# A hybrid S5 / convolution / mLSTM layer: first modulation weights loaded and multiplied ahead of the tokens' statistics, and the moves of the S5 inputs made steps of the S5 side job

## The chip, the core and the metric

The kernel runs on one core of one Trainium2 chip. The metric is the device time of a run in microseconds, and of several runs the median. A second measure is the span of one profiled execution, from its first to its last instruction.

Five engines work side by side, each through its own list of instructions in order: TensorE (PE in the rows, its weight loads PEld), VectorE (DVE), ScalarE (ACT), GpSimd (POOL) and SyncE (SP). SP and POOL only issue loads here, apart from a few clears. An instruction that waits holds up all that stands behind it on its engine.

## The reference, cut to what matters

One layer of a backbone with 256 latent tokens `x` and 256 context tokens `ctx`, each of 2048 features:

```
sh1, sc1, g1, sh2, sc2, g2 = split(silu(c) @ w_mod + b_mod, 6)      # for x with c, for ctx with c_ctx
hx = rmsnorm(x) * (1 + sc1) + sh1 ; hc the same of ctx              # statistics: mean of squares per token
zx = hx @ w_in + b_in ; zc = hc @ w_in + b_in                       # columns: S5, convolution, q, k, v, o, gates
mix = concat(s5_mixer(zc, zx), conv_module(zx), mlstm_mixer(zc, zx))
x = x + g1 * (mix @ w_out)
x = x + g2 * (swiglu(rmsnorm(x) * (1 + sc2) + sh2) @ w_ffn_out)
return rmsnorm(x)
```

The S5 mixer is a diagonal recurrence in two directions over 32 groups of 16 channels, first over the context, then over the tokens, with a GELU and a gated projection behind it. All inputs are float32.

## The kernel before

**Weights.** All weights of the matrix products are cut into tiles of 128 x 128 and stored in the order in which they are used, in chunks of eight tiles, 512 KB each. `raw_dma` (line 259) loads a chunk on SP into one of three `raw` buffers. `split` writes a high part `whi` (a cast by ScalarE, `acopy`, line 201) and the low rest `wlo` (a subtraction by VectorE, `tt`, line 168); there are three buffers of each. Every product is made of three matmuls (`mm3`): high with high, high with low, low with high. `nxt` hands out the tiles in order, fetches and splits ahead, and calls the planner. In the prediction, "`raw` 0" is the first chunk.

**The start.** SP loads the packed vectors (`pv`, `lam`), an identity (`cst`), the tokens `xr` (line 338) and the context `cr` (line 340) in four loads of 512 KB each, and then what the list `plan` says: the modulation weights of the first row tiles, `wm`, and the first weight chunks, by when they are needed. A row tile's modulation has four pieces of 512 KB. `wm_dma` (line 331) places piece number n in buffer n modulo 7: four buffers `wm` and three borrowed from tiles that are idle then (`wmu`, `wmt`, named for what lies there later). Pieces 0 to 6 are loaded by SP, later ones by POOL, and each of those has to wait until TensorE has multiplied the piece that lay in its buffer. `matvec_piece` multiplies a piece with the SiLU of the two condition vectors, `matvec_end` copies the sums out of PSUM (ScalarE), turns them with two transposes and adds them up into the shift and scale `as1` of one row tile (VectorE).

The statistics: ScalarE squares the tokens (two halves for each load), VectorE adds the two halves, TensorE adds over partitions by a matmul with ones into one bank (`stp`, tag `qk`), and `rsqrt` follows: a logarithm and an exponential on ScalarE and three VectorE operations (`stt`, line 179) that end in `rst`. `make_h` multiplies a row tile of tokens by `rst` and writes `hx` and `hc`, each as high and low part. Beside all this VectorE works through the S5 parameters (`wmt`, `LW`, `LC`, `s5c` in the rows), a side job of small operations.

**Phase 1** goes over the 16 row tiles. For each it multiplies the S5 columns and three tiles of the keys' columns for both streams, and in between makes the modulation and `h` of the next row tile. At its end ScalarE reads four PSUM banks out into `zT` (S5 inputs, features on partitions) and three into `kT` (keys).

**The S5 part.** `U` holds the S5 inputs in chunk layout. `s5_moves` fills it from `zT` by 16 copies of 32 partitions, eight on ScalarE and eight on VectorE (`vcopy`, line 183), written out at once before the S5 side job is added. `s5_job` prepares sixteen pairs of units (`prep`) and runs them (`main5`). `prep` transposes `Wb` (line 839) into a PSUM bank, copies it to `Wi`, then computes `M2` in another bank. `main5` multiplies `U` with `Wi`, scans on VectorE, and ends with matmuls of which the last reads `U` and `M2`. Behind the sixteenth pair come a GELU over `U`, sixteen ScalarE and sixteen VectorE copies into `gT` and a split into `gs`.

**What sets the order.** `Sched` writes TensorE's main work in order and slips steps of the side jobs in between: convolution, S5, attention, gates and the modulations that wait (`mod_job`; a few of these multiply on TensorE, `wm` with `cs`, and are turned at line 749). A side job is a generator, each `yield` ends a step, and `pump` starts steps by priority as long as the rough costs counted for VectorE and ScalarE are less than 3500 ns ahead of TensorE's. The framework then orders the instructions of each engine by its own estimate, except where the order is pinned, and puts in the waits. PSUM has three banks of tag `b`, which the convolution, the modulations, the S5 job and attention share.

Of the kernel before, what the change touches and what calls it, by code (L numbers as in the profile page):

```python
# [19 lines left out]
KT = 16  # L20
# [86 lines left out]
class Sched:  # L107
    """Emits the tensor engine's main work in order and slips steps of side jobs in between."""
# [42 lines left out]
def hybrid_layer_kernel(ctx: ExitStack, tc: tile.TileContext, xt, ctxt, wm1, wmr, wst, wg, bvrow, pvd, cstd, s5p, out):  # L151
# [155 lines left out]
    def rsqrt(o, ps, n, scale, eps, epsv):  # L307
        """o = 1/sqrt(ps*scale + eps), refined by one Newton step"""
# [25 lines left out]

    xr = pre.tile([128, KT, NT], F32, name="xr", tag="X")
# [7 lines left out]
    def load_gates():  # L343
# [5 lines left out]
    # the order of the loads that share the queue up to the end of phase 1: by when they are needed  # L349
    NP1 = (4 + KHEAD) * KT // CH  # L350
    plan = sorted([(8 * c / 7 - RAW_EARLY, 0, c) for c in range(NP1)] +
                  [(i // 4 - (MV_LEAD + 1) / 7 + (i % 4) * 0.01 if i >= 4 else -99, 1, i) for i in range(4 * KT)])
# [51 lines left out]

    lnexp()
    stp = bank("qk", 2)
# [11 lines left out]
    for q in range(4):  # L418
        matvec_piece(0, q)
        plan_pump()  # L420
    matvec_end(0)

# [18 lines left out]
    def s5_params():  # L441
# [43 lines left out]
        # half-angle sine and cosine  # L485
# [17 lines left out]
        # lambda_bar - 1 and its quotient by lambda  # L503
# [15 lines left out]
        # powers of lambda_bar  # L519
# [126 lines left out]
    def fourA(n, src, ps):  # L646
        """column tiles in turn, each over all rows: x tokens only"""
        for kt in range(KT):
            mm3(ps, nxt(), (src[:, kt, 0, :], src[:, kt, 1, :]), kt == 0, kt == KT - 1)
# [7 lines left out]
    def conv_job():  # L657
# [14 lines left out]
        def sum4(x):  # L672
            """sums over partitions and the four tiles, every partition the same"""
# [98 lines left out]
    U = pre.tile([128, 16, 128], F32, name="U", tag="U")  # L772
    def s5_moves():
        for s in range(4):
            for q in range(4):
                o = U[32 * s:32 * s + 32, q::4, :]
                i = zT[32 * q:32 * q + 32, :, s::4]
                if (s + q) % 2:
                    vcopy(o, i)
                else:  # L780
                    acopy(o, i)

    def s5_job():
# [111 lines left out]

        yield from prep(0)
        for p in range(16):
            a, b = main5(p), (prep(p + 1) if p < 15 else iter(()))
# [27 lines left out]
    s5_moves()  # L926
# [3 lines left out]
    # the convolution's columns  # L930
# [15 lines left out]
    def gates_job():  # L946
# [28 lines left out]
        # context columns: decay to the end of the context  # L975
# [204 lines left out]
    # last range, with the sums of squares for the second norm  # L1180
    A2 = sb.tile([128, 16], F32, name="A2")
    stt(A2, mods[:, 2, :], 1.0, pvc("n2g", 0, 16), OP.add, OP.mult)
    class SumSq:
        """sums of squares over features, every partition the same: four tiles at once while there is time"""
# [111 lines left out]
    for n in (1, 1, 2, 2, 2, 2, 2, 2, 2):  # L1296
# [3 lines left out]
        i += n  # L1300


# [1 line left out]
def pack(inp):  # L1304
    f = {k: np.asarray(v) for k, v in inp.items()}

# [103 lines left out]
```

## Time and profile before

| | |
|---|---|
| median of 3 runs | 1482.44 us (1481.68 to 1483.52) |
| span of the profiled execution | 1479.6 us (its own time beside the span is not listed) |
| TensorE busy | 1437.5 us, 97% |
| VectorE busy | 1005.1 us, 68% |
| ScalarE busy | 716.0 us, 48% |
| GpSimd busy | 107.2 us, 7% |
| chain that ended last | TensorE 89%, VectorE 5%, ScalarE 3%, DMA 1% |
| moved by the DMA engines | 315.56 MB, 213 GB/s on average |

TensorE is the engine that sets the time over nearly all of the span; its busy time is a sum over pipelined matmuls. In a timeline, a row is a group of like instructions that follow each other: where it starts, how long the group takes, engine, line, what is written and read, and how many. Brackets at the end give the engine's idle time ahead of the row and what ended it. A row of loads gives the time from issue to landing in its last column.

### The profile page before, as it was taken

How to read it: one execution, taken by the hardware profiler on the slowest of the kernel's cores; microseconds unless marked ns; L12 is line 12 of the kernel's file. 1: busy time of each engine (PE TensorE's matmuls, PEld its weight loads, DVE VectorE, ACT ScalarE, POOL GpSimd, SP SyncE). 2: the span in 40 equal slices, each digit the busy share in tenths (PEclk: the TensorE clock that was granted, in tenths of full speed). 3: DMA queues.
4: the chain of work that ended last, by engine and by line, in shares of the span. 5: the costliest groups of instructions: out<-in, count | busy, mean ns of one | idle time of the engine just before them, and what ended most of it. 6: DMA issues, size and time to landing. Idle time of an engine off the chain costs nothing.

```text
span 1479.6 us, 29243 instructions
## 1 busy us (share of the span) xinstructions
PE 1437.5 (97%) x11840; PEld 1351.2 (91%) x11840; DVE 1005.1 (68%) x1960; ACT 716.0 (48%) x1199; POOL 107.2 (7%) x207
## 2 busy tenths in 40 slices
PE   5999899999999999999899999999999999999996
PEld 3888788887888999999899999999999999999996
DVE  7555699988978887888776677455454554455554
ACT  4334776653565555645544444433444334443353
POOL 1221111110101110011000010000000000000000
PEclk9999999999999999999999999999999999999998
DMA  9997464442526666789477787555565555555553
GB/s 360 368 354 291 160 219 136 162 163 86 169 88 228 214 217 227 268 304 353 143 234 265 282 299 239 183 185 186 183 185 185 188 189 181 188 185 186 185 177 114
DMA packets 87943, 315.56 MB, mean 213 GB/s; under 512 B 10096, under 2 KB 10880, under 8 KB 87808
## 3 DMA queue, kind: packets, MB, share of 16 engines
q1 hardware_dynamic: 60912, 216.67, 44.1%
q0 software_dynamic: 26896, 97.02, 18.4%
q8 instruction: 93, 1.52, 0.4%
q14 instruction: 42, 0.34, 0.1%
HBM read 311.55 MB, written 2.10 MB: 212 GB/s over the span
## 4 chain that ended last, share of the span: by engine, by line
PE 89%; DVE 5%; ACT 3%; DMA 1%; issue 1%; SPq 0%; DVEq 0%; ACTq 0%
PE ps_m L208 70%; PE ps_b L208 13%; PE ps_qk L208 5%; DVE tmp L168 1%; DMA tmp<-in_wg_dram 1%; ACT tmp L195 0%; DMA raw<-in_wst_dram 0%; PE ps_b L839 0%; ACT whi L201 0%; ACT U L201 0%; DVE wlo L168 0%; DMA xr<-in_xt_dram 0%; ACT gT L201 0%; PE ps_b L749 0%; DVE tmp L191 0%
## 5 line engine op out<-in xcount | busy, mean ns | idle before, releaser
L168 DVE TENSOR_TENSOR wlo<-raw,whi 128x1024 fp32r<-128x1024 f32 x386 | 471.6, 1223 | 317.7 <-ACT whi L201 309.5
L201 ACT CAST whi<-raw 128x1024 fp32r<-128x1024 f32 x386 | 404.0, 1047 | 508.6 <-PE ps_m L208 373.8
L208 PE MATMUL ps_m<-h,whi 128*128 128x256 f32 x2624 | 470.4, 282 | 3.6 <-ACT h L195 3.6
L208 PEld LDWEIGHTS ps_m<-h,whi 128*128 128x128 f32 x2624 | 404.1, 189 | 4.0 <-ACT h L195 4.0
L208 PE MATMUL ps_m<-h,wlo 128*128 128x256 f32 x1312 | 370.0, 282 | 0.0
L208 PE MATMUL ps_m<-ffa,whi 128*128 128x256 f32 x1408 | 251.0, 281 | 0.0
L208 PEld LDWEIGHTS ps_m<-h,wlo 128*128 128x128 f32 x1312 | 247.8, 189 | 0.0
L208 PEld LDWEIGHTS ps_m<-ffa,whi 128*128 128x128 f32 x1408 | 215.7, 188 | 1.4 <-issue 1.2
L208 PE MATMUL ps_m<-ffa,wlo 128*128 128x256 f32 x704 | 197.2, 280 | 0.0
L208 PE MATMUL ps_m<-hx,whi 128*128 128x256 f32 x960 | 186.8, 290 | 5.5 <-ACT hx L195 3.6
L208 PEld LDWEIGHTS ps_m<-hx,whi 128*128 128x128 f32 x960 | 148.8, 190 | 24.8 <-issue 16.3
L179 DVE SCALAR_TENSOR_TENSOR macc<-wm,cs,macc 128x512 f32<-128x512 f32 x180 | 134.3, 746 | 6.6 <-ACT macc L195 5.1
L208 PE MATMUL ps_m<-hx,wlo 128*128 128x256 f32 x480 | 135.9, 284 | 0.0
L208 PEld LDWEIGHTS ps_m<-ffa,wlo 128*128 128x128 f32 x704 | 132.2, 188 | 0.0
L331 POOL DMA_DIRECT2D wm<-in_wmr_dram x128 | 67.5, 528 | 614.6 <-DVE macc L179 432.9
L208 PEld LDWEIGHTS ps_m<-hx,wlo 128*128 128x128 f32 x480 | 90.9, 190 | 0.2 <-DVE wlo L168 0.2
L179 DVE SCALAR_TENSOR_TENSOR xres<-ps_m,mods,xres 128x256 f32<-128x256 f32 x96 | 46.1, 481 | 35.0 <-PE ps_m L208 34.8
L179 DVE SCALAR_TENSOR_TENSOR XB<-XB,pv 128x256 f32<-128x256 f32 x120 | 53.7, 479 | 0.6
L208 PE MATMUL ps_m<-hc,whi 128*128 128x256 f32 x256 | 52.0, 284 | 0.0
L208 PE MATMUL ps_m<-mixm,whi 128*128 128x256 f32 x256 | 47.3, 286 | 0.0
L208 PE MATMUL ps_m<-whi,hx 128*128 128x512 f32 x128 | 46.5, 400 | 0.0
L201 ACT CAST ffa<-tmp 128x256 fp32r<-128x256 f32 x44 | 17.7, 405 | 49.6 <-DVE tmp L168 49.6
(267 smaller groups left out, 1997.3 us busy)
## 6 DMA issues: line engine op xcount, KB each, us to landing
raw<-in_wst_dram SPq DMA_DIRECT2D x386, 512.0 KB, 4.1
wm<-in_wmr_dram POOLq DMA_DIRECT2D x128, 512.0 KB, 5.2
wm<-in_wm_dram POOLq DMA_DIRECT2D x32, 512.0 KB, 7.2
wmu<-in_wm_dram POOLq DMA_DIRECT2D x16, 512.0 KB, 7.0
wmt<-in_wm_dram POOLq DMA_DIRECT2D x7, 512.0 KB, 6.4
wm<-in_wm_dram SPq DMA_DIRECT2D x5, 512.0 KB, 10.5
xr<-in_xt_dram SPq DMA_DIRECT2D x4, 512.0 KB, 6.6
cr<-in_ctxt_dram SPq DMA_DIRECT2D x4, 512.0 KB, 9.8
```

Of the source, the lines that this page charges most:

```text
L168: V.tensor_tensor(out=o, in0=a, in1=b, op=op)
L179: V.scalar_tensor_tensor(o, a, s, b, op0=op0, op1=op1)
L201: S.copy(o, a)
L208: i = P.matmul(o, lhsT=l, rhs=r, start=start, stop=stop, skip_group_check=sgc, **kw)
L331: i = (q or nc.gpsimd).dma_start(wm[key], src)
```

## The change

It has two parts. In the first, the loads of the four modulation pieces of row tile 0 are issued on SP ahead of the tokens, the planner's list starts with piece 4, and the multiplication of the four pieces and `matvec_end(0)` are written ahead of the statistics. The call of `plan_pump` behind each piece becomes one call behind all four. In the second, `s5_moves` becomes a generator `s5_move(q)` that makes four of the sixteen copies, with a `yield` behind each two and an extra 500 ns counted for each ScalarE copy; the S5 job runs `s5_move(0)` before the first preparation and `s5_move(1)` to `s5_move(3)` ahead of the first three pairs. The rest of the diff removes comments.

```diff
+    for q in range(4):
+        wm_dma((0, q), wm1[0, q], nc.sync)
     xr = pre.tile([128, KT, NT], F32, name="xr", tag="X")
     cr = sb.tile([128, KT, NT], F32, name="cr", tag="R1")
...
     plan = sorted([(8 * c / 7 - RAW_EARLY, 0, c) for c in range(NP1)] +
-                  [(i // 4 - (MV_LEAD + 1) / 7 + (i % 4) * 0.01 if i >= 4 else -99, 1, i) for i in range(4 * KT)])
+                  [(i // 4 - (MV_LEAD + 1) / 7 + (i % 4) * 0.01 if i >= 4 else -99, 1, i) for i in range(4, 4 * KT)])
...
+    for q in range(4):
+        matvec_piece(0, q)
     lnexp()
+    matvec_end(0)
+    plan_pump()
     stp = bank("qk", 2)
...
     rsqrt(rst, stp, 512, 1.0 / D, eps6, 1e-6)
-    for q in range(4):
-        matvec_piece(0, q)
-        plan_pump()
-    matvec_end(0)
-
...
-    def s5_moves():
+    def s5_move(q):
         for s in range(4):
-            for q in range(4):
-                o = U[32 * s:32 * s + 32, q::4, :]
-                i = zT[32 * q:32 * q + 32, :, s::4]
-                if (s + q) % 2:
-                    vcopy(o, i)
-                else:
-                    acopy(o, i)
+            o = U[32 * s:32 * s + 32, q::4, :]
+            i = zT[32 * q:32 * q + 32, :, s::4]
+            if (s + q) % 2:
+                vcopy(o, i)
+            else:
+                acopy(o, i)
+                sc.act += 500
+            if s % 2:
+                yield
...
+        yield from s5_move(0)
         yield from prep(0)
         for p in range(16):
+            if p < 3:
+                yield from s5_move(p + 1)
             a, b = main5(p), (prep(p + 1) if p < 15 else iter(()))
...
-    s5_moves()
     s5o = {}
     s5j = sc.add(s5_job(), P_S5)
```

The order of the built program moves in four places that matter here. The first is SP's queue at the start. Before, tokens and context stand ahead of the first modulation pieces:

```order
L231 DMA pv<-in_pvd_dram 128x377
L233 DMA lam<-in_pvd_dram 128x96
L235 DMA cst<-in_cstd_dram 128x128
L338 DMA xr<-in_xt_dram 128x1024 x4
L340 DMA cr<-in_ctxt_dram 128x1024 x4
L331 DMA wm<-in_wm_dram 128x1024 x4
L259 DMA raw<-in_wst_dram 128x1024
```

In the change:

```order
L231 DMA pv<-in_pvd_dram 128x377
L233 DMA lam<-in_pvd_dram 128x96
L235 DMA cst<-in_cstd_dram 128x128
L331 DMA wm<-in_wm_dram 128x1024 x4
L340 DMA xr<-in_xt_dram 128x1024 x4
L342 DMA cr<-in_ctxt_dram 128x1024 x4
L259 DMA raw<-in_wst_dram 128x1024
```

The four `wm` moved ahead of eight loads, which each come four places later; the first `raw` keeps its place.

The second is ScalarE behind the squares at the start, where the first activation of `ps_qk` is the logarithm of the statistics and the next the exponential. Before:

```order
L195 ACTIVATE tmp<-ps_qk,kc 128x512
L195 ACTIVATE tmp<-tmp 128x512
L201 COPY tmp<-ps_b 128x256
L201 CAST whi<-raw 128x1024
L195 ACTIVATE hx<-tmp,as_209 128x256
L195 ACTIVATE hc<-tmp,as_209 128x256
```

In the change:

```order
L195 ACTIVATE tmp<-cr 128x512 x8
L201 CAST whi<-raw 128x1024
L195 ACTIVATE tmp<-ps_qk,kc 128x512
L195 ACTIVATE tmp<-tmp 128x512
L195 ACTIVATE hx<-tmp,as_134 128x256
L195 ACTIVATE hc<-tmp,as_134 128x256
```

The modulation's copy went ahead of the squares, and the first cast stands ahead of the logarithm.

The third is ScalarE at the end of phase 1, from the last reading of `zT` on. Before:

```order
L195 ACTIVATE zT<-ps_qk,pv 128x512
L195 ACTIVATE kT<-ps_qk,bks 128x512
L201 COPY U<-zT 32x4x128
L195 ACTIVATE kT<-ps_b,bks 128x512 x2
L201 COPY U<-zT 32x4x128 x7
L201 CAST whi<-raw 128x1024 x2
L201 COPY Mb<-tmp 64x20x16
```

In the change, from the second reading of `kT` on, and the stretch up to the copies of `Wi` and `M2`:

```order
L195 ACTIVATE kT<-ps_b,bks 128x512 x2
L201 COPY U<-zT 32x4x128
L201 CAST whi<-raw 128x1024
L201 COPY Mb<-tmp 64x20x16
L195 ACTIVATE tmp<-cst,s5c 128x128
L201 COPY U<-zT 32x4x128
L195 ACTIVATE tmp<-tmp,kc 128x256
L201 CAST whi<-raw 128x1024
```

```order
L201 CAST whi<-raw 128x1024
L201 COPY Wi<-ps_b 128x512
L201 COPY U<-zT 32x4x128 x3
L201 COPY M_1945<-ps_b 128x128
L201 CAST whi<-raw 128x1024
```

The seven copies in a row are spread: five of the eight now stand ahead of the copy of `Wi`, with four casts and the S5 preparation between them, and three behind it. VectorE's eight copies stay in a row in both.

The fourth is TensorE in the last chunk of the values, whose matmuls are 512 wide, around the last matmul of the S5 job, that of `U` and `M2`. Before:

```order
L208 MATMUL ps_m<-whi,hx 128x512
L208 MATMUL ps_m<-wlo,hx 128x512
L208 MATMUL ps_b<-tmp,Mb 128x64
L208 MATMUL ps_m<-whi,hx 128x512
L208 MATMUL ps_b<-tmp,Mb 128x64 x3
L208 MATMUL ps_b<-U,M_5171 128x64
L208 MATMUL ps_m<-whi,hx 128x512
```

In the change, where four transposes of a modulation and the queries' first matmuls (256 wide) follow:

```order
L208 MATMUL ps_qk<-whi,hc 128x512
L208 MATMUL ps_b<-tmp,Mb 128x64 x4
L208 MATMUL ps_b<-U,M_5258 128x64
L208 MATMUL ps_qk<-wlo,hc 128x512
L208 MATMUL ps_qk<-whi,hc 128x512
L750 MATMUL ps_b<-cst,macc 128x128 x4
L208 MATMUL ps_m<-hx,whi 128x256 x2
```

The job's last matmul moved from the beginning of that chunk to two matmuls before its end.

## Rows read from the trace of the kernel before

**Rows 1.** The page: busy time of TensorE, and the chain by engine.
```profile
PE 1437.5 (97%) x11840; PEld 1351.2 (91%) x11840; DVE 1005.1 (68%) x1960; ACT 716.0 (48%) x1199; POOL 107.2 (7%) x207
...
PE 89%; DVE 5%; ACT 3%; DMA 1%; issue 1%; SPq 0%; DVEq 0%; ACTq 0%
```
**Rows 2.** Timeline of TensorE, first main matmul: start us, us, instruction, idle before.
```profile
28.58 1.01 PE L208 MATMUL ps_m<-hx,whi 128*128 128x256 f32 x3 [3.60 <-ACT hx L195]
```
**Rows 3.** Timeline of TensorE around the end of phase 1.
```profile
146.67 0.40 PE L208 MATMUL ps_b<-hx,whi 128*128 128x256 f32 x2
...
149.61 1.07 PE L208 MATMUL ps_b<-wm,cs 128*32 128x512 f32 x8
...
157.80 0.80 PE L208 MATMUL ps_b<-hx,whi 128*128 128x256 f32 x2 [4.08 <-ACT whi L201]
```
**Rows 4.** Timeline of TensorE at the end of the S5 job.
```profile
450.19 0.39 PE L208 MATMUL ps_b<-U,M 128*128 128x64 f32 x2
...
455.36 0.40 PE L208 MATMUL ps_m<-hx,whi 128*128 128x256 f32 x2
...
463.17 0.50 PE L208 MATMUL ps_m<-hx,whi 128*128 128x256 f32 x2 [1.71 <-ACT whi L201]
```
**Rows 5.** Busy time in three stretches (columns in the first line).
```profile
core 0: us, PE busy (x) PEld busy (x) DVE busy (x) ACT busy (x) POOL busy (x), PEclk, DMA share, GB/s
36.00:140.00 104.00, 102.97 (x1075) 87.88 (x1074) 57.37 (x152) 35.69 (x59) 27.37 (x53) 1.00 0.95 356
158.00:164.00 6.00, 6.00 (x24) 4.11 (x25) 3.79 (x4) 5.73 (x12) 0.00 (x0) 0.57 0.61 196
462.00:468.00 6.00, 4.83 (x22) 4.35 (x23) 6.00 (x9) 1.49 (x3) 0.53 (x1) 0.72 0.65 208
```
**Rows 6.** Single loads, issued at 6.03, 11.58, 13.04, 19.41, 23.10 and 45.00 us.
```profile
cr<-in_ctxt_dram SPq DMA_DIRECT2D x1, 512.0 KB, 10.8
...
wm<-in_wm_dram SPq DMA_DIRECT2D x1, 512.0 KB, 10.4
...
raw<-in_wst_dram SPq DMA_DIRECT2D x1, 512.0 KB, 10.2
...
raw<-in_wst_dram SPq DMA_DIRECT2D x1, 512.0 KB, 12.5
...
wm<-in_wm_dram POOLq DMA_DIRECT2D x1, 512.0 KB, 7.0
...
raw<-in_wst_dram SPq DMA_DIRECT2D x1, 512.0 KB, 6.6
```
**Rows 7.** Timeline of POOL: its first loads of `wm`.
```profile
23.10 2.08 POOL L331 DMA_DIRECT2D wm<-in_wm_dram  x4 [20.09 <-PE ps_b L208]
```
**Rows 8.** Timeline of ScalarE at the start.
```profile
6.34 1.15 ACT L195 ACTIVATE tmp<-xr 128x512 f32<-128x512 f32 x2 [0.22 <-DMA xr<-in_xt_dram]
...
22.24 0.69 ACT L195 ACTIVATE tmp<-ps_qk,kc 128x512 f32<-128x512 f32 x1 [2.75 <-PE ps_qk L208]
...
24.39 1.05 ACT L201 CAST whi<-raw 128x1024 fp32r<-128x1024 f32 x1
27.93 0.60 ACT L195 ACTIVATE hx<-tmp,as 128x256 fp32r<-128x256 f32 x1 [2.49 <-DVE as L175]
```
**Rows 9.** Timeline of VectorE at the start.
```profile
7.52 0.69 DVE L168 TENSOR_TENSOR tmp<-tmp 128x512 f32<-128x512 f32 x1 [0.18 <-ACT tmp L195]
...
20.34 0.68 DVE L168 TENSOR_TENSOR tmp<-tmp 128x512 f32<-128x512 f32 x1
...
25.33 0.69 DVE L179 SCALAR_TENSOR_TENSOR rst<-tmp 128x512 f32<-128x512 f32 x1
...
26.81 0.42 DVE L168 TENSOR_TENSOR tmp<-cr,rst 128x256 f32<-128x256 f32 x1
```
**Rows 10.** Timeline of ScalarE at the end of phase 1.
```profile
148.85 7.82 ACT L201 COPY U<-zT 32x512 f32<-32x512 f32 x7
156.70 1.99 ACT L201 CAST whi<-raw 128x1024 fp32r<-128x1024 f32 x2
```
**Rows 11.** Timeline of ScalarE behind the last pair of the S5 job.
```profile
452.22 6.89 ACT L201 COPY gT<-U 32x128 f32<-32x128 f32 x16
```

## The prediction

> **What bounds the kernel now.** I read the page first: TensorE's busy time and the chain that ended last [rows 1]. TensorE is busy for 1437.5 of 1479.6 us and holds 89% of the chain, so a change can only move the few places where it stands idle, or open new ones. Next I read TensorE's timeline and looked for a number in brackets at a row's end, which is idle time ahead of that row with the engine that ended it. Three such places lie in the code that the diff touches: the first main matmul at 28.58 us, after 3.60 us of idleness ended by ScalarE's `hx` [rows 2]; the row at 157.80 us, after 4.08 us ended by a `whi` cast [rows 3]; and the row at 463.17 us, after 1.71 us ended by a `whi` cast too [rows 4]. For each I then read the timeline of the engine named, to see what stood ahead of the releaser. Phase 1 behind the first main matmul has next to no idle time (TensorE busy for 103 of 104 us from 36 on [rows 5]), so a later start there moves everything after it by the same amount.
>
> **The start: what has to land.** A load's landing is its issue plus its time to landing [rows 6]. The last context load `cr` lands at 6.03 + 10.8 = 16.8 us, the last of the four `wm` at 11.58 + 10.4 = 22.0, and `raw` 0 at 13.04 + 10.2 = 23.2. Four loads lie between the first two, so a load of 512 KB takes (22.0 - 16.8) / 4 = 1.3 us when the DMA engines are full. The diff swaps the two groups on SP's queue: the four `wm` come ahead of the eight token loads, and the last `cr` takes the place of the last `wm`, 22.0, which is 5.2 later. `raw` 0 keeps its place in the queue.
>
> The diff moves something else too. POOL loads the next four `wm` into the buffers of the first four, so it waits for TensorE to have multiplied those. In before that released it at 23.10 us, after 20.09 us of idleness [rows 7]. Now the first four land where the `xr` did, from 6.3 us on [rows 8], so POOL issues its four loads between about 7 and 13 us, in the middle of the token loads. Whether they overtake them is the largest unknown of this case. One row speaks for it: POOL's first load, issued at 23.10, landed at 30.1, ahead of the `raw` that SP had issued at 19.41, which took 12.5 us and landed at 31.9 [rows 6]. One speaks against: the `raw` of 45.00 took only 6.6 us among several loads of POOL [rows 6]; if POOL's loads are served in the order of arrival, two of them go ahead of the last `cr` and three ahead of `raw` 0. With none ahead the last `cr` lands at 22.0; in order of arrival at 24.6, and `raw` 0 at 27.1; with all four ahead at 27.1, and `raw` 0 at 28.3. I take four, by the row at 23.10, since it shows the same four loads against a full SP queue.
>
> The Trainium skill (DMA: Bandwidth & Descriptors, section Queues, rings and completion order) says that a DMA engine takes turns between the queues that have work for it, packet by packet. By that rule POOL's loads get half of the engines as soon as they are issued, all four go ahead, and the start is the one that I take; the row at 23.10 agrees with it, and the one at 45.00 only in part.
>
> **The start: from the last load to TensorE.** In before, the squares of the first `xr` begin at 6.34 us, when it has landed, and VectorE's sum of the two halves ends at 7.52 + 0.69 = 8.2, so 1.9 after landing [rows 8, 9]. The last of these sums ran at 20.34, ended at 21.0, and the logarithm followed at 22.24, 1.2 later [rows 8, 9]. That last sum stood 3.5 us behind the last landing, because VectorE was working off the S5 parameters between the sums; with later loads that work is done before, and this is what the new order gives back. From landing to logarithm it is then 1.9 + 1.2 = 3.1, and the logarithm runs at 27.1 + 3.1 = 30.2. In the new ScalarE order the `whi` cast of `raw` 0 stands ahead of the logarithm; it ends at 28.3 + 1.05 = 29.4 [rows 8] and is not last. From logarithm to TensorE it took 28.58 - 22.24 = 6.3. In it `rst` was done at 25.33 + 0.69 = 26.0 and the products with the tokens at 26.81 + 0.42 = 27.2, but `hx` began only at 27.93 [rows 8, 9]: small copies and the reduction of the modulation stood between. They are done earlier now, which saves some 1.5 with the gaps between the steps ahead of `rst`; 4.8 remain. TensorE starts at 35.0, which is 6.4 later. In before VectorE put `wlo` ahead of the low half of `hx`, and TensorE stood again after its first matmuls; in the new order `wlo` is done sooner, and I put 0.4 to its credit. So the start costs **+6.0**; +4.0 in order of arrival (logarithm at 27.1 + 1.05, TensorE at 33.0), and +0.9 with none ahead (25.1, then 29.9). The multiplications themselves cost nothing either way: they run while TensorE waits for tokens. The low clock at the start stays as it is, since TensorE stands idle ahead of its first main matmul in both.
>
> **The moves into `U`.** In before seven of ScalarE's eight copies run from 148.85 to 156.67, 1.12 each, and the `whi` cast behind them comes at 156.70 [rows 10]. TensorE stands 4.08 us [rows 3], and from 158 to 164 the granted clock is 0.57, which loses 6 x 0.43 = 2.6 more [rows 5]. That is 6.7 us to be had. In the new order the cast stands behind two copies, six copies or 6.7 us earlier, so this wait goes. What is late next: `M2` takes the PSUM bank of the `Wi` transposes, the third of the tag `b` (convolution and modulation hold the others), and stands in TensorE's order seven matmuls behind them, with the rest of a weight chunk behind it. It waits for ScalarE's copy of `Wi`. Ahead of that copy, from 148.85 on, stand four `U` copies (4.5), four casts (4.2), the small steps of the S5 preparation (about 4.0: ScalarE's 5.73 of the six microseconds from 158 less some 1.7 of casts [rows 5]) and a table and the copy itself (about 1): 162.5. TensorE gets there after three chunks of 2.9 (146.67 to 149.61), 1.1 for the modulation and about 2 for transposes, the seven matmuls and a short wait for its first bank [rows 3]: 146.7 + 11.8 = 158.5. It would stand 3 to 4 us, and with the low clock behind it lose about 5.7 in all where it lost 6.7. I take **-1.0**, between -6.7 (the `Wi` copy isn't last) and +0.5. VectorE's eight copies stay in a row, and cost nothing as long as its next `wlo` waits for the cast.
>
> **The end of the S5 job.** The moves add eight steps to the job's planned course, and its last matmul (`U`,`M2`) slips. In before it ends at 450.6, early in the last chunk of the values: about 5.0 us of that chunk follow, up to 455.36, and two chunks of 2.9 [rows 3, 4], so TensorE had 10.8 us to do while ScalarE ran GELU, sixteen copies into `gT` (6.89 [rows 11]) and casts; it waited 1.71. In the new order it stands two matmuls ahead of that chunk's end. ScalarE's chain behind it is about as long (12.5 from 450.6 to the cast that TensorE waited for; one cast has moved ahead of it, and the reading out of a modulation and a query row have come in). TensorE has 0.5, four transposes and three chunks to do, about 9.6. The wait grows from 1.7 to some 3.3, and the clock, 0.72 from 462 to 468 [rows 5], costs some 0.9 more than before. I take **+2.5**, from 0 to +6.0 (each of the waits there in full, with a low clock behind it).
>
> **The sum.** 6.0 - 1.0 + 2.5 = +7.5. The profiled execution spans 1479.6, and the median of the runs, 1482.44, lies 2.8 above it, time outside the span, which the change doesn't touch. So 1479.6 + 7.5 + 2.8 = **1489.9 us**; with the bounds of the start alone 1485 to 1490.
>
> **The rivals.** (a) The stall at the `U` copies goes and leaves no successor: -6.7, with nothing at the end of the S5 job and the tokens unhindered by POOL, +0.9. Together -5.8, 1476.6, faster. For it speaks that the cast is the only releaser the trace names at 157.80; against it the waiting `M2`. It decides for faster once the start costs less than 3.7. (b) POOL's loads go in order of arrival, +4.0, TensorE loses half as much at the moves, -4.0, and the end costs +1.0: 1483.4, no difference. For it speaks the `raw` of 45.00. (c) The start as forecast, the stall at the moves only changes its name, +0.5, and the end of the S5 job costs its upper bound: 6.4 + 0.5 + 6.0 = +12.9, 1495.3. For it speaks that ScalarE's chain there is the longest of the kernel in one piece. That the change doesn't do what it says holds for half of the second part: by the order, VectorE's copies are not spread.
>
> **How the numbers follow.** I give my forecast 0.53, with 1486 to 1493 of its own, (a) 0.12, (b) 0.20 and (c) 0.15. A measurement of this kernel tells 0.2%, or 3.0 us, from no change: faster is below 1479.5, slower above 1485.4. So faster 0.12, the same 0.20, slower 0.68. The range leaves out most of (a) and the far end of (c): 1480.5 to 1495.5.
>
> **What would show it.** The last `cr` landing near 27, POOL's first four `wm` issued before 14 us, the logarithm near 30 and the first main matmul near 35 would show the first step right; `cr` at 22 and a start near 30 would show it wrong. A wait of TensorE for `Wi` where it waited for `whi` shows the second, and a wait of 3 us or more for `RH` or `whi` behind the `gT` copies the third. The forecast is wrong if phase 1 makes up for a late start, or if the moved steps put a wait where TensorE has none now.

## The result, and the profile after

The changed kernel takes 1495.54 us (median of four runs, 1493.43 to 1496.81), the kernel before 1482.06 beside it: a ratio of 1.0091, with an interval of 1.0077 to 1.0105. It is slower, as forecast, but by 13.5 us where 7.5 were forecast, and it lies 0.04 above the range's upper end. Run once more later (after_again), the same kernel took 1493.61 (1.0075, 1.0058 to 1.0093), with the same waits. All figures are of fast executions; one slow execution each of e16_best_squares (3460.92 us) and e20_both_paces (1748.81 us) is left out of them.

The page of the changed kernel: TensorE's busy time and the chain by engine.

```profile
span 1491.7 us, 29212 instructions
...
PE 1441.7 (97%) x11840; PEld 1352.3 (91%) x11840; DVE 1004.8 (67%) x1960; ACT 712.9 (48%) x1197; POOL 107.6 (7%) x207
...
PE 88%; DVE 4%; ACT 4%; DMA 3%; issue 1%; SPq 0%; DVEq 0%; ACTq 0%
```

Against [rows 1] TensorE is busy for 4.2 us more with the same 11840 matmuls, so some of them ran slower, and the chain holds 3% of DMA where it held 1%. Where that comes from is read in the chain's pieces in order of time; the first two of the long ones are:

```profile
3.55 7.79 DMA wm<-in_wm_dram
11.35 15.48 DMA cr<-in_ctxt_dram
```

The last `cr` lands at 11.35 + 15.48 = 26.83 us, where it landed at 16.8 [rows 6]. Four timelines of the changed kernel show the start that follows from it (start us, us, instruction, idle time ahead). POOL's first loads, from 8.88 us on instead of 23.10 [rows 7]:

```profile
8.88 0.53 POOL L331 DMA_DIRECT2D wm<-in_wm_dram  x1 [5.87 <-DMA wm<-in_wm_dram]
...
12.79 0.53 POOL L331 DMA_DIRECT2D wm<-in_wm_dram  x1 [0.74 <-PE ps_b L208]
```

Single loads issued at 10.1 and 12.8 us (the last column is us from issue to landing):

```profile
cr<-in_ctxt_dram SPq DMA_DIRECT2D x1, 512.0 KB, 15.5
...
raw<-in_wst_dram SPq DMA_DIRECT2D x1, 512.0 KB, 15.5
wm<-in_wm_dram POOLq DMA_DIRECT2D x1, 512.0 KB, 11.7
```

So POOL's fourth load, issued at 12.79, landed at 24.5, and the third `cr`, issued at 10.08 ahead of it, at 25.6: all four of POOL's went ahead of the last two `cr`. ScalarE's logarithm and TensorE's waits:

```profile
30.02 0.69 ACT L195 ACTIVATE tmp<-ps_qk,kc 128x512 f32<-128x512 f32 x1 [0.84 <-PE ps_qk L208]
```
```profile
34.77 1.26 PE L208 MATMUL ps_m<-hx,whi 128*128 128x256 f32 x4 [4.78 <-ACT hx L195]
...
168.21 2.56 PE L208 MATMUL ps_b<-Mb,Wb 128*32 128x128 f32 x32 [3.19 <-ACT Wi L201]
...
251.56 0.46 PE L998 MATMUL ps_b<-cst,rows 64*128 64x64 f32 x4 [2.34 <-DVE mods L187]
...
475.40 1.39 PE L208 MATMUL ps_qk<-RH,kT 128*128 128x256 f32 x4 [3.65 <-ACT RH L195]
...
479.54 0.58 PE L208 MATMUL ps_m<-hx,wlo 128*128 128x256 f32 x1 [0.86 <-DVE wlo L168]
```

The 3.60 us of [rows 2] became 4.78 at a start that is 6.2 later. The 4.08 for `whi` of [rows 3] is gone, and 3.19 for `Wi` stands in its place. The 1.71 of [rows 4] became 3.65 + 0.86. The wait at 251.56, at the gates, has no row in before. Busy times and granted clock behind two of these waits:

```profile
168.00:176.00 8.00, 7.79 (x71) 7.41 (x72) 2.20 (x5) 6.01 (x8) 0.00 (x0) 0.79 0.47 145
476.00:483.00 7.00, 6.14 (x24) 4.88 (x23) 6.40 (x9) 4.63 (x6) 1.05 (x2) 0.51 0.51 167
```

To place the 12.1 us between the two spans, I cut both traces at the same main matmuls (those with `whi` or `wlo`, counted from the first) and took, for each stage, TensorE's idle time plus its busy time times one minus the granted clock:

| Stage | ends at, before and after (us) | lost before | lost after | difference |
|---|---|---|---|---|
| up to the first main matmul | 28.58, 34.77 | | | +6.2 (later) |
| phase 1 (600 matmuls) | 138.13, 143.60 | 3.6 | 3.3 | -0.2 |
| moves into `U` (to 800) | 175.49, 179.43 | 6.8 | 5.4 | -1.4 |
| gates (to 1500) | 328.93, 331.90 | 1.6 | 3.4 | +1.7 |
| end of the S5 job (to 2400) | 553.30, 568.61 | 3.7 | 8.1 | +4.4 |
| to 3600 | 721.51, 733.44 | 9.0 | 9.6 | +0.5 |
| rest | 1479.6, 1491.7 | 11.7 | 11.7 | 0.0 |

That makes 11.2 of 12.1; 0.9 has no place in it. (The ends at the 2400th matmul lie 15.3 us apart because more side work stands ahead of it in the changed kernel; "lost" leaves that out.) The size of the start holds to about 1 us: four kernels that start like before (e2, e8, e9 and e19 below) have their first main matmul at 27.40 to 27.85, and e6, which starts like the changed kernel, at 33.95. The start and the moves came out as forecast, the end of the S5 job cost almost twice its term, and the gates stand in no term at all.

### The profile page after: what moved, and what is told of

Same layout as the page of the kernel before. It is cut to its first block, busy times and chain, and to the rows that moved or that the text cites. A ratio compares the mean times of both kernels' runs of the same rounds, so it can differ in the third digit from the quotient of the medians.

```text
span 1491.7 us, 29212 instructions
## 1 busy us (share of the span) xinstructions
PE 1441.7 (97%) x11840; PEld 1352.3 (91%) x11840; DVE 1004.8 (67%) x1960; ACT 712.9 (48%) x1197; POOL 107.6 (7%) x207
## 4 chain that ended last, share of the span: by engine, by line
PE 88%; DVE 4%; ACT 4%; DMA 3%; issue 1%; SPq 0%; DVEq 0%; ACTq 0%
PE ps_m L208 70%; PE ps_b L208 12%; PE ps_qk L208 5%; DVE tmp L168 1%; DMA cr<-in_ctxt_dram 1%; ACT tmp L195 1%; DMA tmp<-in_wg_dram 1%; ACT whi L201 1%; DMA wm<-in_wm_dram 1%; DMA raw<-in_wst_dram 0%; PE ps_b L842 0%; ACT gT L201 0%; DVE wlo L168 0%; DVE tmp L191 0%; ACT U L201 0%
## 5 line engine op out<-in xcount | busy, mean ns | idle before, releaser
L208 PE MATMUL ps_b<-wm,cs 128*32 128x256 f32 (+1 forms) x424 | 42.7, 468 | 8.1 <-DVE wmt L173 7.5
## 6 DMA issues: line engine op xcount, KB each, us to landing
cr<-in_ctxt_dram SPq DMA_DIRECT2D x4, 512.0 KB, 15.5
```

Source lines behind the costliest of these rows:

```text
L208: i = P.matmul(o, lhsT=l, rhs=r, start=start, stop=stop, skip_group_check=sgc, **kw)
```

## The experiments

Times are medians; each ratio is to runs of the kernel before on the same chip. One profile can lie some 3 us off its kernel's median, so sizes are read from medians, and places from traces.

### The two parts alone

e1_start_only is the changed kernel with `s5_moves()` as before; e2_moves_only is the kernel before with the moves as steps:

```
 def s5_job():
+    yield from s5_move(0)
     yield from prep(0)
     for p in range(16):
+        if p < 3:
+            yield from s5_move(p + 1)
...
-s5_moves()
```

> The first part alone: loads and multiplication of the first pieces ahead of the tokens, all sixteen moves in one go as before. Theory (the two parts add up, the start is one loss of its own): last cr lands near 26.8, first main matmul at 34.8, and the whole is about 6 us slower than before, near 1488. Rival (a late start shifts loads against everything that follows, so most of the 13 us come from it): 1492 or more, with new waits behind phase 1.

> The second part alone: tokens first as before, the moves as steps of the S5 job. Theory: first main matmul at 28.6 as before; the wait for whi at the end of phase 1 is replaced by one for Wi of about 3 us (1 to 1.5 us won), a wait of about 2 us comes at the gates near 245, and 3 to 4 us more are lost behind the gT copies; about 5 to 7 us slower than before, 1487 to 1489. Rival (the moves cost nothing by themselves): within 2 us of before.

The start alone takes 1487.35 (1.0039, 1.0025 to 1.0053), the moves alone 1489.26 (1.0045, 1.0031 to 1.0060), beside 1482.41. Together 4.9 + 6.9 = 11.8 of the 11.9 to 13.5 that the two runs of the full change gave: the parts add up, and the larger one is the moves, which the forecast had at +1.5. TensorE's timelines, first of the start alone, then of the moves alone:

```profile
34.81 1.26 PE L208 MATMUL ps_m<-hx,whi 128*128 128x256 f32 x4 [4.78 <-ACT hx L195]
...
164.16 0.80 PE L208 MATMUL ps_b<-hx,whi 128*128 128x256 f32 x2 [4.07 <-ACT whi L201]
...
469.18 0.50 PE L208 MATMUL ps_m<-hx,whi 128*128 128x256 f32 x2 [1.71 <-ACT whi L201]
```
```profile
163.13 2.77 PE L208 MATMUL ps_b<-Mb,Wb 128*32 128x128 f32 x32 [3.19 <-ACT Wi L201]
...
247.03 0.46 PE L997 MATMUL ps_b<-cst,rows 64*128 64x64 f32 x4 [2.34 <-DVE mods L187]
...
470.94 2.08 PE L208 MATMUL ps_qk<-RH,kT 128*128 128x256 f32 x4 [3.65 <-ACT RH L195]
```

The start moves everything by some 6 us and leaves the later waits at the 4.08 and 1.71 of [rows 3, 4]. The three other waits belong to the moves, to a hundredth of a microsecond.

### What in the moves costs it: the steps, or the time counted for them

The diff does two things there. It makes the copies steps of the job, and each copy on ScalarE now adds 500 ns to ScalarE's planned time (`sc.act += 500`, eight times, 4.0 us). The planner issues no step of any side job while that planned time is too far ahead of TensorE's. Without the line it counts 190 + 0.84 x 512 = 620 ns for such a copy (`acopy`), with it 1120; the copies take 1.12 us each [rows 10]. So the line makes the count true to the trace. e6_no_500 is the changed kernel without the line, e8_moves_no_500 is e2_moves_only without it, and e9_count_500 is the kernel before with the line alone, in `s5_moves()`, with no instruction added:

```
                 acopy(o, i)
-                sc.act += 500
```

> The changed kernel without the extra 500 ns that each ScalarE move counts in the planner; the eight steps stay. Theory (the counted 500 ns, not the eight steps, make the S5 job late): the last matmul of U and M2 comes 28 main matmuls earlier, 9 before that of the kernel before; the waits behind the gT copies shrink from 4.5 to 2 us or less, and 3 to 4 us are won against the changed kernel: 1491 to 1492. Rival (the steps themselves make it late): 1495 as the changed kernel.

> The second part alone without the counted 500 ns: tokens first as before, moves as eight steps of the S5 job. Theory (the spread moves win at the end of phase 1 and lose only through the 500 ns): first main matmul at 28.6, no wait of over 1 us at the gates, the end of the S5 job as in the kernel before; 2 to 4 us faster than before, 1478 to 1480. Rival (spreading the moves costs by itself): slower than before.

> The kernel before, all moves in one go, with nothing added but the 500 ns counted for each ScalarE move, 4 us of the planner's ScalarE time. Theory (the count alone makes the S5 job late): the first pair's last matmul comes 145 main matmuls later, the last one's 9 later; waits at the gates or behind the gT copies grow, 3 to 7 us slower than before. Rival (the count harms only together with the steps): within 2 us of before.

| Pair, without and with the counted time | medians | difference |
|---|---|---|
| e6_no_500 and the changed kernel | 1484.50, 1495.54 | 11.0 |
| e8_moves_no_500 and e2_moves_only | 1478.54, 1489.26 | 10.7 |
| before and e9_count_500 | 1481.11, 1490.93 | 9.8 |

The ratios are 1.0011 (1.0001 to 1.0021) for e6, 0.9981 (0.9971 to 0.9991) for e8 and 1.0072 (1.0052 to 1.0093) for e9. The runs of the first two pairs were not beside each other. Taken each against the kernel before beside it, the first differs by 9.9 to 11.4 us (after_again, and the changed kernel at first) and the second by 9.4. So in three surroundings the counted time alone costs 9 to 11 us, more than all else in the change and more than was expected of e6 (3 to 4) and of e9 (3 to 7). As steps, without it, the moves are worth 2.6 us. In e6 the eight steps stand in the order, and the last wait is nearly as long as in before, 1.82 us for 1.71, though VectorE's `vx` ends it there and not a cast:

```profile
462.99 0.48 PE L208 MATMUL ps_m<-hx,whi 128*128 128x256 f32 x2 [1.82 <-DVE vx L168]
```

What the count does is seen in the order of TensorE's instructions. The last `U`,`M2` matmul stands behind 1899 main matmuls in before, behind 1890 in e6 and behind 1918 in the changed kernel; in e9 the first pair's moved from 840 to 985. Other side work moves with it, and so other waits appear. In e9, with the copies where before has them, these are:

```profile
157.84 0.80 PE L208 MATMUL ps_b<-hx,whi 128*128 128x256 f32 x2 [4.73 <-ACT whi L201]
...
207.74 1.80 PE L208 MATMUL ps_b<-Mb,Wb 128*32 128x128 f32 x32 [2.33 <-issue]
...
466.52 1.11 PE L749 MATMUL ps_b<-cst,macc 128*128 128x128 f32 x4 [3.34 <-DVE macc L179]
```

Only part of the 11 us has a place. Between the profiles of e6 and of the changed kernel, the gates' stage accounts for 1.4 (2.0 against 3.4 lost) and the end of the S5 job for 4.5 (3.6 against 8.1). The rest of the spans' 7.3 lies in small pieces of either sign or has no place, and their medians lie 3.7 further apart than their spans. How the shifted plan makes the rest of the 11 us isn't shown.

### What the wait for `Wi` hangs on

Without the count the 3.19 us for `Wi` are still there. I had put it down to ScalarE: four `U` copies, casts, small steps and a table load stand ahead of the `Wi` copy. In the changed kernel ScalarE's timeline shows the end of that row:

```profile
162.13 1.14 ACT L201 COPY U<-zT 32x512 f32<-32x512 f32 x1
163.28 1.28 ACT L195 ACT_TABLE_LOAD   x1
...
166.55 1.03 ACT L201 CAST whi<-raw 128x1024 fp32r<-128x1024 f32 x1
167.49 0.57 ACT L201 COPY Wi<-ps_b 128x512 f32<-128x512 f32 x1
```

e19_moves_vector takes the copies of three of the four groups away from ScalarE, on top of e8, and counts ScalarE's 620 for each as the copy there did, so that the order of all else is nearly kept:

```
             if (s + q) % 2:
                 vcopy(o, i)
+            elif q:
+                V.tensor_copy(o, i)
+                sc.act += 620
             else:
                 acopy(o, i)
```

> e8_moves_no_500 with ScalarE's moves of q = 1 to 3 on VectorE, counted in the plan as before. Theory (the wait of 3.2 us ahead of M2 is ScalarE's copy of Wi standing behind five U copies): the copy of Wi comes 3 to 4 us earlier, the wait shrinks to under 0.5 us and the low clock behind it goes; 3 to 5 us faster than e8, 1474 to 1476. Rival (the wait is the casts' and the table's): it stays above 2 us.

It takes 1476.16 us (0.9957, 0.9942 to 0.9972), which beats both kernels; e8's interval only just touches this one. The stretch from 150 to 170 us, in e8 and then in e19 (busy time of PE, PEld, DVE, ACT, POOL, then clock, DMA share, GB/s):

```profile
150.00:170.00 20.00, 16.81 (x145) 15.25 (x145) 8.32 (x14) 16.96 (x25) 1.05 (x2) 0.91 0.60 202
```
```profile
150.00:170.00 20.00, 19.12 (x174) 16.59 (x173) 16.20 (x33) 12.61 (x23) 2.32 (x5) 1.00 0.60 205
```

TensorE does 174 matmuls where it did 145, at full clock, and its wait for `Wi` is 0.34:

```profile
160.10 1.80 PE L208 MATMUL ps_b<-Mb,Wb 128*32 128x128 f32 x32 [0.34 <-ACT Wi L201]
```

The stage to 800 main matmuls loses 1.4 us in e19, 5.4 in e8 and in the changed kernel, and 6.8 in before. So the waiting was ScalarE's, and nothing else was late there. Part of the win goes again: at the end of the S5 job e19 waits for a `wlo`, which e8 doesn't.

```profile
458.68 0.39 PE L208 MATMUL ps_m<-hx,wlo 128*128 128x256 f32 x1 [2.77 <-DVE wlo L168]
```

A copy of this shape takes 1.12 us on ScalarE [rows 10] and 5.03 / 8 = 0.63 on VectorE, which has idle time in this stretch. VectorE's eight copies in before:

```profile
146.14 5.03 DVE L183 COPY U<-zT 32x512 f32<-32x512 f32 x8 [1.78 <-ACT zT L195]
```

### The start: POOL's loads, or what stands behind the last landing

The forecast had two prices here: +6.0 if POOL's loads overtake the tokens, +0.9 if not. e3_pieces_on_sp puts POOL's first four loads on SP's queue, behind the tokens, in the changed kernel; e23_start_on_sp does so in e1_start_only:

```
-wm_dma(divmod(i, 4), wm1[i // 4, i % 4], nc.sync if i < NWX or i >= WMQ else None)
+wm_dma(divmod(i, 4), wm1[i // 4, i % 4], nc.sync if i < NWX + 4 or i >= WMQ else None)
```

> The changed kernel with pieces 7 to 10 of the modulation weights on SP's queue, behind the first weight chunk, in place of POOL's. Theory (POOL's four loads overtake the tokens): last cr lands at 22.0 and not at 26.8, first main matmul near 30, 5 us less than the changed kernel: about 1490. Rival (the order on SP alone makes the start late): last cr near 26.8 still, 1495.

> The first part alone (e1_start_only) with modulation pieces 7 to 10 on SP behind the first weight chunk, in place of POOL's; nothing else. Theory (POOL's overtaking is 2.4 us of the 6.2, the later place of the tokens on SP the other 3.8): first main matmul near 32.4, about 3.5 us slower than before, so 2 us faster than e1_start_only. Rival (what POOL's loads cost is given back elsewhere, as the time of e3_pieces_on_sp suggests): about 5 us slower than before, as e1_start_only.

In e3 the last `cr` lands at 10.67 + 11.1 = 21.8, 5.0 earlier, as expected. But TensorE starts only at 32.42, and the time is 1495.47 (1.0084, 1.0064 to 1.0104), no better than with POOL's loads ahead; what its trace lost again behind the start stands in the last section. In e23 it starts at 32.53 and takes 1485.75 (1.0020, 1.0008 to 1.0031), 1.6 less than e1 by medians, though the two intervals overlap. So POOL's overtaking makes 2.3 of the 6.2 us at the start (34.77 to 32.42, 34.81 to 32.53), and the tokens' later place on SP's queue the other 3.9. My +0.9 for that was wrong. VectorE's timeline of e3 shows why; the sums of two squares run 1.7 us apart, with the S5 parameters between them:

```profile
18.08 0.69 DVE L168 TENSOR_TENSOR tmp<-tmp 128x512 f32<-128x512 f32 x1
18.69 0.18 DVE L168 TENSOR_TENSOR wmt<-wmt 128x32 f32<-128x32 f32 x1
...
19.64 0.18 DVE L168 TENSOR_TENSOR wmt<-wmt 128x32 f32<-128x32 f32 x1
19.81 0.69 DVE L168 TENSOR_TENSOR tmp<-tmp 128x512 f32<-128x512 f32 x1
...
25.77 0.69 DVE L168 TENSOR_TENSOR tmp<-tmp 128x512 f32<-128x512 f32 x1 [0.93 <-ACT tmp L195]
```

Loads land 1.3 apart and sums run 1.7 apart, so the last sum, at 25.77, is 4.0 behind the last landing, and the logarithm, at 27.68, is 5.9 behind. Two things can hold the sums: VectorE's parameters in between, and the four `tmp` buffers, two for each pair of squares, which ScalarE must wait to get back. e13_params_late loads `lam` behind the tokens, so the parameters can't begin earlier; e15_own_squares gives the squares buffers of their own; e20_both_paces does both. All three have the start of e23.

```
-    nc.sync.dma_start(lam, pvd[:, NPV:])
...
         nc.sync.dma_start(cr[:, 4 * q:4 * q + 4, :], ctxt[:, 4 * q:4 * q + 4, :])
+    nc.sync.dma_start(lam, pvd[:, NPV:])
```
```
-            sq, s2 = tmp(), tmp()
+            sq, s2 = sqb[:, 8 * half + 2 * q, :], sqb[:, 8 * half + 2 * q + 1, :]
```

> The first part alone, with modulation pieces 7 to 10 on SP as in e3_pieces_on_sp, and the load of the S5 parameters' input (lam) behind the tokens, so that VectorE takes up the parameters after the sums. Theory (in e3 the last sum came 4 us behind the last landing because VectorE worked off the parameters first): last cr near 22, last sum done 2 us behind it, logarithm at 25, first main matmul at 29.7, 2.7 earlier than in e3; about 1 us slower than before. Rival (VectorE isn't what holds the sums): first main matmul at 32.4 as in e3, 4 us slower than before.

> The first part alone, modulation pieces 7 to 10 on SP as in e3_pieces_on_sp, and each square of the statistics in a buffer of its own in place of four tmp buffers in turn. Theory (the sums are paced by the ring of four buffers, some 1.7 us for each load against 1.3 of landing, so the logarithm follows the first landing by about 16 us): with buffers of their own the logarithm comes 3 to 4 us behind the last landing, so near 25.5 where the last cr lands at 22, and the first main matmul near 30.3, 2 us earlier than in e3. Rival (VectorE's parameter work holds the sums): last sum 4 us behind the last landing as in e3, first main matmul near 32.4.

> The first part alone with modulation pieces 7 to 10 on SP, own buffers for the squares (as e15_own_squares) and the load of lam behind the tokens (as e13_params_late). Theory (the ring of four buffers and VectorE's parameters each hold the sums at 1.5 to 1.7 us for a load, so that lifting one shows the other): with both lifted the logarithm follows the last landing by 3 to 3.5 us, where it was 5.2 to 5.9 in e3, e13 and e15, and the first main matmul by about 8. Rival (a third thing holds the sums): still 5 us or more.

| Kernel | last `cr` lands | logarithm | behind | first main matmul | time, ratio |
|---|---|---|---|---|---|
| e23_start_on_sp | 21.88 | 27.79 | 5.9 | 32.53 | 1485.75, 1.0020 |
| e13_params_late | 20.44 | 25.67 | 5.2 | 30.41 | 1483.45, 1.0012 (1.0002 to 1.0021) |
| e15_own_squares | 20.93 | 26.36 | 5.4 | 31.11 | 1485.99, 1.0026 (1.0016 to 1.0035) |
| e20_both_paces | 20.97 | 24.17 | 3.2 | 28.92 | 1485.62, 1.0020 (1.0008 to 1.0033) |
| after | 26.83 | 30.02 | 3.2 | 34.77 | 1495.54, 1.0091 |

Either alone changes the distance little, since the other still holds the sums; both together bring the logarithm to 3.2 behind the landing, my 3.1. VectorE's sums in e20, 1.3 apart in the steady part:

```profile
18.28 0.69 DVE L168 TENSOR_TENSOR sqb<-sqb 128x512 f32<-128x512 f32 x1 [0.73 <-ACT sqb L195]
19.53 0.69 DVE L168 TENSOR_TENSOR sqb<-sqb 128x512 f32<-128x512 f32 x1 [0.55 <-ACT sqb L195]
20.81 0.69 DVE L168 TENSOR_TENSOR sqb<-sqb 128x512 f32<-128x512 f32 x1 [0.59 <-ACT sqb L195]
```

In the changed kernel POOL's loads stretch the landings so far that the sums keep up, which is why 3.1 held there (in e1, with the same start, it was 4.1). e20 starts only 0.3 later than before's trace (1.1 to 1.5 later than e2, e8, e9 and e19) and still takes 3 to 4 us more than before. Its trace is 3.9 longer: 0.3 at the start, 1.4 in phase 1 (5.0 lost against 3.6), 0.4 up to the 3600th main matmul and 1.7 behind it, nearly all of it in matmuls that follow each other more slowly (last section).

e10_loads_first changes only the order of the loads, in the kernel before:

```
+    for q in range(4):
+        wm_dma((0, q), wm1[0, q], nc.sync)
     xr = pre.tile([128, KT, NT], F32, name="xr", tag="X")
```

> The kernel before with nothing changed but SP's order: the first four modulation pieces ahead of the tokens; in the code the multiplication stays behind the statistics. Theory (the order of the loads alone makes the start late): first main matmul near 34.8, 5 to 6 us slower than before, 1487 to 1488, as e1_start_only. Rival (the place of the multiplication does): within 2 us of before.

1490.02 (1.0050, 1.0031 to 1.0069), with the last `cr` at 26.89 and the first main matmul at 36.05: the loads make the start late, and multiplying ahead of the logarithm gives 1.3 us of it back (36.05 to 34.8).

### Versions that start earlier

e14_best and e16_best_squares are e8 with one of the two paces taken away, in the load order of before; e22_start_and_moves is e19 with both.

> The best of what the runs suggest: tokens first as before, the load of lam behind them, moves as steps without the counted 500 ns. Theory (VectorE's parameters hold the sums in the kernel before too): logarithm near 20 in place of 22.2, first main matmul near 25.5, and with the win at the moves 5 to 7 us faster than before, 1475 to 1477. Rival (the modulation pieces or the first weight chunk are next to come late): first main matmul at 27 or later, as e8_moves_no_500 within 1.5 us.

> e8_moves_no_500 (tokens first, moves as steps, no counted 500 ns) with each square in a buffer of its own. Theory of the ring: logarithm at 20 to 21 in place of 22.2, first main matmul about 1 us earlier than in e8, so 1 us faster. Rival (VectorE's work between the sums, the parameters, sets the pace there): the same as e8_moves_no_500 within 1 us.

> e19_moves_vector with own buffers for the squares and the load of lam behind the first modulation pieces; tokens first as before. Theory (in the kernel before too the ring and the parameters hold the sums): logarithm near 20, first main matmul near 26, so 1 to 2 us faster than e19, 1474 to 1475. Rival (the modulation pieces, landing at 22, and the first weight chunk are next): first main matmul at 27.5 or later, and the same time as e19.

e14 takes 1477.86 (0.9975, 0.9963 to 0.9988) and e16 1480.88 (0.9990, 0.9979 to 1.0001). Both gain less than expected: e14 was to be 5 to 7 us faster than before, and e16 1 us faster than e8 (0.9981). In e14 the logarithm comes at 21.44, but the parameters now stand behind it on VectorE, and the first main matmul comes at 28.32; in e16 the sums still run 1.7 apart and it comes at 27.71. In e22 both fall away, and TensorE starts earliest of all:

```profile
24.94 1.01 PE L208 MATMUL ps_m<-hx,whi 128*128 128x256 f32 x3 [2.34 <-ACT hx L195]
...
37.88 0.64 PE L208 MATMUL ps_b<-wmu,cs 128*32 128x256 f32 x8 [0.51 <-DMA wmu<-in_wm_dram]
```

Yet it takes 1477.05 (0.9957, 0.9940 to 0.9974), no less than e19, which started at 27.40. The 600th main matmul ends the lead: 137.63 in e22, 137.66 in e19. Phase 1 lost 6.0 us instead of 4.4, in pieces of which the wait for `wmu` is the longest, while the DMA engines are busy throughout (share 1.03 from 25 to 45 us, 407 GB/s; 0.99 in e19 from 27 to 47, 0.95 later in before [rows 5]). A later start moved phase 1 as a whole; an earlier one seems to meet loads that haven't landed, of which the 0.51 us alone are shown.

### The changed kernel once more

after_again is the changed kernel, unaltered.

> The changed kernel once more, beside the others of this call, to compare its time and its waits with those of the variants on the same chip. Theory: 12 to 14 us slower than before, first main matmul at 34 to 35, waits of 3.2 us for the copy of Wi, 2.3 at the gates, and 4.5 behind the gT copies. Rival (part of the 13 us was a matter of the first chip): 9 us or less.

Its waits are 3.18, 2.33, 3.62 and 1.11, its first main matmul 34.77, its span 1491.5. So the places and the lengths of the waits named above are no accident of one execution. The low clock behind them varies: the end of the S5 job lost 7.1 us here and 8.1 at first, since the clock was low for half as long.

## Where the prediction held, and which step failed

**The start** was right in size (+6.2 less 0.2 given back in phase 1, for +6.0; by e1's median 4.9), and its marks were right in the changed kernel: POOL's loads all issued before 14 us, the last `cr` near 27, the logarithm near 30, TensorE near 35. The choice of "all four ahead" held. By the Trainium skill (DMA: Bandwidth & Descriptors, section Queues, rings and completion order) an engine takes turns between the queues that have work. This trace agrees: the last `cr` needed 15.5 us with POOL's loads beside it and 11.1 in e3 without them. What didn't hold is the share. I put 5.1 us on POOL, as the distance between two landings, and the runs show 2.3, because the logarithm follows the slower of two things, the landings and the sums. The step "later loads that work is done before, and this is what the new order gives back" is right only if POOL's loads are ahead.

**The moves** were right: -1.4 for -1.0, the wait for `whi` gone, 3.19 for `Wi` where 3 to 4 were worked out, low clock behind it. e19 confirms the ScalarE row that the working counted up.

**The end of the S5 job** is the step that failed, in its cause and in its size. It was "the moves add eight steps to the job's planned course, and its last matmul slips". It does slip, and it did stand two matmuls ahead of the chunk's end, but not for the steps: e6 has the same steps, and the matmul comes earlier than in before. What slipped it is the time counted for each copy. I had read that line of the diff as bookkeeping and put it at nothing. By medians the whole second part cost 6.9 us where -1.0 + 2.5 = +1.5 stood: -2.6 for the steps and 9.4 for the count. The size at this place was off too: ScalarE's chain, forecast at 12.5 (and 12.5 less TensorE's 9.6 gives a wait of 2.9, not the 3.3 taken), took 13.4, since the row that TensorE waited for was not a cast but `RH`, behind everything:

```profile
466.08 6.84 ACT L201 COPY gT<-U 32x128 f32<-32x128 f32 x16
...
473.33 1.12 ACT L201 CAST gs<-gT 128x512 fp32r<-128x512 f32 x2
...
474.87 0.47 ACT L195 ACTIVATE RH<-ps_m,pv 128x256 f32<-128x256 f32 x1
```

From the end of the last `U`,`M2`, at 461.94, to the end of `RH` at 475.34 are 13.4 us. Then 0.86 for a `wlo` came on top, and seven microseconds at 0.51 of the clock (3.0 lost, where I had 1.7 + 0.9). In all +4.4 for +2.5.

**The gates** had no term. Their transposes take a PSUM bank that VectorE's reduction of a modulation must read out first, and the reduction stood behind scans:

```profile
247.72 3.06 DVE L191 TENSOR_TENSOR_SCAN tmp<-kc,tmp,rows 32x256 f32<-32x256 f32 x4
...
251.35 0.16 DVE L187 TENSOR_REDUCE mods<-ps_b 128x4 f32<-128x16 f32 x1
```

That pairing came from the shifted plan; neither before nor e6 has it. The forecast followed the moved job to its end and not the other jobs that the same planner places. The three terms and the gates make +6.0 - 1.4 + 4.4 + 1.7 = +10.7, with 0.5 further on and 0.9 without a place; by medians +13.5. In time the result is next to rival (c), 1495.3, which had the full upper bound at the end of the S5 job (and the start at 6.4, not at the forecast's 6.0); that is near by luck, since its mechanism, a stall that only changes its name, is half of what happened. Rival (a), no successor to the stall, is what e19 made in that stage.

## What to carry to other kernels

A cost that a planner only counts is as real as an instruction: eight times 500 ns of counted time cost 9 to 11 us and moved waits to places that the diff doesn't touch. The truer count gave the worse order here, so try such a number on its own, and follow every job that the planner places. Where work waits for a row of loads, ask for each row what paces it, the landings or the buffers and engines in between; removing one of two paces shows almost nothing. To get rid of a stall, look at what stands ahead of the releaser on its engine, and whether an engine with idle time does it faster: moving six copies to VectorE gave the lowest median here, with intervals that overlap those of e14 and e22.

## What the hardware showed that was not expected

The same wait can be followed by a low clock or not. The 2.34 us at the gates, with the same instructions around it, left the clock at 1.00 in the changed kernel, in after_again and in e2. In e3 the clock fell to half (1.2 GHz) when TensorE had stood for 1.9 of them, and stayed there for 6.8 us. The eight microseconds from 0.8 ahead of the wait's end on, first in the changed kernel, then in e3:

```profile
250.75:258.75 8.00, 7.19 (x57) 5.95 (x58) 7.83 (x21) 5.72 (x10) 1.05 (x2) 1.00 0.45 140
```
```profile
249.00:257.00 8.00, 7.19 (x36) 6.88 (x36) 6.99 (x19) 2.96 (x6) 0.00 (x0) 0.57 0.29 108
```

With the same busy time TensorE got through 36 matmuls where it got through 57, and the stage of the gates lost 6.7 us in e3 and 3.4 in the changed kernel. That is why a wait of 2 us should be given a range that has the low clock in it.

It isn't what made e3 no faster, though: at the 3600th main matmul its trace is 0.5 us ahead of the changed kernel again (732.94 against 733.44), and it ends 3.6 behind. Nearly all that it loses there is lost without a wait (TensorE's idle time is 11.9 against 11.7) and at full clock: the same matmuls follow each other more slowly. A stretch of before, of e3 and of e20; the changed kernel has the 2110 matmuls of before:

```profile
850.00:1100.00 250.00, 250.00 (x2110) 250.00 (x2109) 146.37 (x171) 104.76 (x141) 6.33 (x12) 1.00 0.64 209
```
```profile
850.00:1100.00 250.00, 250.00 (x2086) 250.00 (x2085) 145.21 (x169) 104.26 (x145) 6.33 (x12) 1.00 0.63 209
```
```profile
850.00:1100.00 250.00, 250.00 (x2105) 250.00 (x2103) 145.85 (x170) 105.77 (x148) 6.36 (x12) 1.00 0.64 209
```

From the 3600th main matmul to the end, 13 of the 18 traces take 758.1 to 758.7 us. The four kernels whose squares have buffers of their own (e15, e16, e20, e22) take 759.5 to 760.3, each 1.4 to 1.8 more than the like kernel without them (e23, e8, e13, e19), and e3 takes 762.3. So that edit costs some 1.5 us far from its place, which is part of why e16, e20 and e22 gained so little. What makes the matmuls slower there, and whether e3's other executions have it too, isn't shown.
